# Expert gates of a PEER layer: one-hot products on TensorE replaced by indirect adds into DRAM tables

## The chip, the cores and the metric

The kernel runs on one core of a Trainium2 chip. The metric is the device time of one execution in microseconds (us), the median of several runs. An engine is a processor of the core with its own instruction queue: TensorE (PE, with its weight loads as PEld), VectorE (DVE), ScalarE (ACT), GpSimd (POOL) and SyncE (SP). SP and POOL also issue DMAs, which run on the core's 16 DMA engines.

## What is computed

Three layers in turn each end in a PEER feed-forward block over 256 tokens of width 1024. The rest of a layer (convolution, RWKV, gated linear attention, memory attention, norms) is not touched by the change. The block, cut to what matters:

```python
q = (xb @ w_q).reshape(TOK, 8, 2, 128)                   # 8 heads, 2 halves
s = einsum('thcd,hcnd->thcn', q, sub_keys)               # 128 sub-keys a half
top_s, top_i = top_k(s, 16)
best_s, best_c = top_k((top_s[:,:,0,:,None] + top_s[:,:,1,None,:]).reshape(TOK, 8, 256), 16)
e = i1 * 128 + i2                                        # 8 x 16 experts of 16384 for a token
gate = softmax(best_s)                                   # within a head
act = gelu(einsum('td,ted->te', xb, expert_u[e]))
y = einsum('te,ted->td', gate * act, expert_v[e])
```

An expert may be chosen by several heads of one token; its gates then add up. Within one head the 16 experts are distinct. All values are float32.

## The kernel before, in words

Instead of fetching chosen experts, the kernel multiplies all 16384 experts: 128 blocks of 128 experts. The function `peer` runs, for each layer, three stages:

- The query stage: 16 blocks of `w_q` are streamed (`pq`), scores are formed on PE (`pscore`) and copied to `S`.
- The up stage: a loop over 128 blocks `b` of `uT`. Each step streams 512 KB, splits it into a high and a low part (`hi` on ACT, L75; `lo` on DVE, L77), does 24 matmuls into `pu` (L91 to L93), and puts Gelu of the result into `C3[:, b]`, a table of 128 (expert in block) x 128 blocks x 256 tokens in SBUF.
- The down stage: a loop over 128 blocks of `v` (`vstep`, then `acc_nat`). Each step streams 512 KB, splits it the same way, splits `C3[:, b]` into `ch` (ACT, L86) and `cl` (DVE, L87), and does 12 matmuls of 512 columns into `py` (L142 to L144).

The gates are made by a generator, `background`, which runs beside the query and the up stage. Each piece of it yields a planned cost, and `pull(rate)` is called once a streamed block (14 times in the query stage, then 128 times in the up stage), adding `rate` = 1.3 to a budget that the pieces use up. First it finds the top 16 of every score row (`topk1`, 32 pieces of cost 1.0), then for each half `tt` of 128 tokens the 128 experts and gates (`topk2`, pieces that sum to 20.0). Then, for each group of four tokens, DVE and ACT build one-hot rows `A` (times the gate) and `B`, and PE multiplies them into a gate plane (`pg`, L1075), which multiplies or fills the columns of those four tokens in `C3` (L1079, L1080).

Streams go through `stream`: SP loads `raw` (4 buffers), then `hi` and `lo` (3 buffers each). The order of instructions on each engine is fixed when the program is built: the framework's scheduler puts an instruction where it expects its inputs to be ready, by priority, so that work of a later stage may stand ahead of work of an earlier one. On the chip an engine then keeps this order and waits where an input is not there. `cst` is a pool of constants, `wp` one of work tiles of `peer`, `dr` one of DRAM tiles. GpSimd does little here: a few loads of rows, stores of results and memsets.

Of the kernel before, what the change touches and what calls it, by code (L numbers as in the profile page):

```python
# [6 lines left out]
F32 = mybir.dt.float32  # L7
# [32 lines left out]
class Net:  # L40
    def __init__(self, ctx, nc, tc):
        self.nc, self.tc = nc, tc
        self.cst = ctx.enter_context(tc.tile_pool(name="cst", bufs=1))
        self.sp = ctx.enter_context(tc.tile_pool(name="sp", bufs=PARTS))
        self.xp = ctx.enter_context(tc.tile_pool(name="xp", bufs=1))
        self.ps = ctx.enter_context(tc.tile_pool(name="ps", bufs=2, space=PSUM))
        iota_i = self.sp.tile([128, 128], I32, tag="raw", name="iota_i", bufs=RAW)
        nc.gpsimd.iota(iota_i, pattern=[[1, 128]], base=0, channel_multiplier=0)
        self.iota = self.cst.tile([128, 128], F32, name="iota")
        nc.vector.tensor_copy(self.iota, iota_i)  # L50
        col_i = self.sp.tile([128, 1], I32, tag="raw", name="col_i", bufs=RAW)
        nc.gpsimd.iota(col_i, pattern=[[0, 1]], base=0, channel_multiplier=1)
        self.col = self.cst.tile([128, 1], F32, name="col")
        nc.vector.tensor_copy(self.col, col_i)
        self.ident = self.cst.tile([128, 128], F32, name="ident")
        self.ready = nc.vector.tensor_scalar(self.ident, self.iota, self.col, None, op0=OP.is_equal)

        self.vec2 = self.mark = None
        self.los = []
        self.eps = {}  # L60
        for e in (RMS_EPS, LN_EPS, GN_EPS):
            t = self.cst.tile([128, 1], F32, name=f"eps{len(self.eps)}")
            nc.vector.memset(t, e)
            self.eps[e] = t
        warm = self.cst.tile([128, 1], F32, name="warm")
        nc.scalar.activation(warm, self.eps[RMS_EPS], AF.Sqrt)


    def stream(self, ap, n=1024):
        nc = self.nc  # L70
        raw = self.sp.tile([128, n], F32, tag="raw", name="raw", bufs=RAW)
        nc.sync.dma_start(raw, ap)
        hi = self.sp.tile([128, n], F32R, tag="hi", name="hi")
        lo = self.sp.tile([128, n], F32R, tag="lo", name="lo")
        nc.scalar.copy(hi, raw)  # L75
        with self.behind():
            self.los.append(nc.vector.tensor_tensor(lo, raw, hi.bitcast(F32), op=OP.subtract))  # L77
        return hi, lo

    def behind(self):  # L80

# [152 lines left out]
    def block1(self, a, xh_out, xl_out, stop=None):  # L234
# [5 lines left out]
        with ExitStack() as ctx:  # L240
# [35 lines left out]
            for n, i in enumerate((4, 5, 6, 7, 12, 13, 0, 1, 2, 3, 8, 9, 10, 11)):  # L276
# [6 lines left out]
                S.activation(zf[:, i], pz, AF.Copy, scale=omu[:, i:i + 1])  # L283
                V.scalar_tensor_tensor(zf[:, i], z[:, 0:272], vc("mu", i), zf[:, i], op0=OP.mult, op1=OP.add)
            r_, k_, v_ = zf[:, 0:4], zf[:, 4:8], zf[:, 8:12]
            with tc.issue_after(self.los[5].ins):
                m = self.bmask(mp, f1)
            h64s = mp.tile([128, 128], F32, name="h64s")
# [735 lines left out]
            po = self.proj_nat(a["b_w_out"], fh, fl_, (6, 7, 0, 1, 2, 3, 4, 5))  # L1024
            self.add_ln(fp, res, po, a, (1, 0), xh_out, xl_out, dst)

    def peer(self, xh, xl, wq, skT, uT, v, rate=1.3, dve_a=2):


        nc, tc = self.nc, self.tc  # L1030
# [2 lines left out]
        with ExitStack() as ctx:  # L1033
# [12 lines left out]
            eq = scr(4096, 1024)  # L1046
            views = [self.topk_views(s_) for s_ in small]

            state = {"ub": 0, "tok": 0}

            def background():
                for g in range(16):
                    for tt in range(2):
                        yield from self.topk1(views[tt], S[tt], tmp, 2 * g + tt)
                idT = []
                for tt in range(2):
                    r = yield from self.topk2(wp, views[tt], cand[tt], tmp, eq)
                    idT.append(r)
                for t0 in range(0, 256, 4):
                    tt = t0 // 128  # L1060
                    t1 = t0 - tt * 128
                    A = wp.tile([128, 4, 128], F32, tag="A", name="A")
                    B = wp.tile([128, 4, 128], F32, tag="B", name="B")
                    pg = self.ps.tile([128, 4, 128], F32, tag="y", name="pg", bufs=4)
                    V.tensor_tensor(B, self.iota[:, None, :].to_broadcast([128, 4, 128]),  # L1065
                                    idT[tt][:, 1, t1:t1 + 4, None].to_broadcast([128, 4, 128]), op=OP.is_equal)
                    for j in range(4):
                        t = t1 + j
                        i1, gg = idT[tt][:, 0, t:t + 1], idT[tt][:, 2, t:t + 1]
                        if j < dve_a:  # L1070
                            V.tensor_scalar(A[:, j], self.iota, i1, gg, op0=OP.is_equal, op1=OP.mult)
                        else:
                            nc.scalar.activation(A[:, j], self.iota, AF.Abs, bias=idT[tt][:, 3, t:t + 1])
                            nc.scalar.activation(A[:, j], A[:, j], AF.Relu, scale=idT[tt][:, 4, t:t + 1], bias=gg)  # L1074
                        nc.tensor.matmul(pg[:, j], B[:, j], A[:, j], start=True, stop=True)  # L1075
                    pT = pg.rearrange("p t b -> p b t")
                    n = state["ub"]
                    if n < 128:
                        nc.scalar.copy(C3[:, n:, t0:t0 + 4], pT[:, n:])  # L1079
                    V.tensor_tensor(C3[:, :n, t0:t0 + 4], C3[:, :n, t0:t0 + 4], pT[:, :n], op=OP.mult)  # L1080
                    state["tok"] = t0 + 4
                    yield 0.6 + 0.26 * dve_a + 0.06 + 0.00416 * n

            bg = background()
            debt = [0.0]
# [16 lines left out]
            def score(g, qT):  # L1102
# [4 lines left out]
                for tt in range(2):  # L1107
                    nc.scalar.copy(S[tt][:, g], pg[:, tt])

            for g in range(16):  # L1110
                hi, lo = self.stream(wq[g])
                if g == PARTS:
                    self.mark = None
                pa = self.ps.tile([128, 512], F32, tag="a", name="pq", bufs=4)
                if g < 2:
                    self.mm8(pa[:, :256], hi, lo, xh, xl)
                else:
                    for c in range(8):
                        s = slice(c * 128, c * 128 + 128)
                        self.mm3(pa[:, :256], hi[:, s], lo[:, s], xh[:, c], xl[:, c], c == 0, c == 7)  # L1120
                if g:
                    score(g - 1, qT)
                qT = wp.tile([128, 256], F32, tag="act", name="qT")
                nc.scalar.copy(qT, pa[:, :256])
                if g > 1:
                    pull(rate)
            score(15, qT)
            for b in range(128):
                pull(rate)
                hi, lo = self.stream(uT[b])  # L1130
                pa = self.ps.tile([128, 512], F32, tag="a", name="pu", bufs=4)
                for c in range(8):
                    s = slice(c * 128, c * 128 + 128)
                    self.mm3(pa[:, :256], hi[:, s], lo[:, s], xh[:, c], xl[:, c], c == 0, c == 7)
                tm = state["tok"]
                if tm < 256:
                    nc.scalar.activation(C3[:, b, tm:], pa[:, tm:256], AF.Gelu)
                if tm > 0:
                    act = wp.tile([128, 256], F32, tag="act", name="act")
                    nc.scalar.activation(act[:, :tm], pa[:, :tm], AF.Gelu)  # L1140
                    V.tensor_tensor(C3[:, b, :tm], C3[:, b, :tm], act[:, :tm], op=OP.mult)
                state["ub"] = b + 1
            pull(1e9)
            py = [self.ps.tile([128, 512], F32, tag="y", name="py", bufs=4) for i in range(4)]
            def vstep(b):
                hi, lo = self.stream(v[b])
                ch = wp.tile([128, 256], F32R, tag="ch", name="ch", bufs=TAIL)
                cl = wp.tile([128, 256], F32R, tag="cl", name="cl", bufs=TAIL)
                self.split(ch, cl, C3[:, b])
# [26 lines left out]
        self.top16(w["tv"][:, g], w["ti"][:, g], S[:, g], tmp[:, (i % 8) * 128:(i % 8) * 128 + 128])  # L1176
        yield 1.0

    def topk2(self, wp, w, cand, tmp, eq):

# [51 lines left out]
        sm = t[:, 0:8]  # L1234
        V.tensor_reduce(sm, gt, axis=AX.X, op=OP.add)
        V.reciprocal(sm, sm)
        V.tensor_tensor(gt, gt, sm[:, :, None].to_broadcast([128, 8, 16]), op=OP.mult)
        pt = self.ps.tile([128, 512], F32, tag="y", name="pt", bufs=4)
        for i in range(3):
            nc.tensor.transpose(pt[:, i * 128:i * 128 + 128], pick[:, i], self.ident)  # L1240
        idT = wp.tile([128, 5, 128], F32, tag="idT", name="idT")
        nc.scalar.copy(idT[:, 0:3].rearrange("p a b -> p (a b)"), pt[:, :384])
        V.tensor_scalar(idT[:, 3], idT[:, 0], -1.0, None, op0=OP.mult)
        V.tensor_scalar(idT[:, 4], idT[:, 2], -1.0, None, op0=OP.mult)
        yield 1.0
        return idT


def blk(w):
# [70 lines left out]
def build(nc, tc, a):  # L1320
    with ExitStack() as ctx:
# [3 lines left out]
        n.dr = dr  # L1325
        hs = [dr.tile([256, 1024], F32, name=f"h{i}") for i in range(3)]
        a["h1"] = hs[0]

        def xt():
            return [n.xp.tile([128, 8, 256], F32R, tag="x" + x, name="x" + x) for x in "hl"]  # L1330

        def peer(l, x):
            return n.peer(*x, a[f"wq{l}"], a[f"sk{l}"], a[f"u{l}"], a[f"v{l}"])
        x = xt()
        n.block1(a, *x)
        nc.gpsimd.dma_start(n.vec2, a["vec2"])
# [36 lines left out]
```

## Time and profile before

| what | value |
|---|---|
| median of 3 runs | 3102.98 us (3101.91 to 3103.67) |
| the profiled execution | 3102.61 us, of which the span of the trace is 3100.8 us |
| PE busy | 3044.2 us (98% of the span) |
| DVE, ACT, POOL busy | 2200.1 us (71%), 1763.2 us (57%), 30.6 us (1%) |
| DMA | 518.33 MB, mean 167 GB/s |

Busy times are of one profiled execution. Matmuls overlap in the engine, so that a matmul's own duration is longer than the time by which it moves the next one; a stretch divided by the count of its matmuls gives the latter.

### The profile page before, as it was taken

To read this page: it belongs to the slowest core of one execution; us is meant where nothing else is said; L and a number is where in the kernel's file an instruction comes from. 1 tells how busy PE (TensorE), PEld (TensorE's weight loads), DVE (VectorE), ACT (ScalarE), POOL (GpSimd) and SP (SyncE) were. 2 spreads that over 40 slices of the span, in tenths; PEclk is the share of its full clock that TensorE was granted. 3 is DMA by queue.
4 is the path that set the end of the run, shared out by engine and by line. 5 is a ranking of instruction groups with operands and counts; after the bars stand their busy time and mean duration, and the time that the engine had idled before them with its cause. 6 is when DMAs were issued, how large, how long until landed. Compare 5 with 4: busy or idle time off the path is not lost.

```text
span 3100.8 us, 57093 instructions
## 1 busy us (share of the span) xinstructions
PE 3044.2 (98%) x22090; PEld 2798.0 (90%) x22090; DVE 2200.1 (71%) x4412; ACT 1763.2 (57%) x3433; POOL 30.6 (1%) x83
## 2 busy tenths in 40 slices
PE   9999999999999999999999999999999999999998
PEld 8888999999888878899999988888889999988887
DVE  6977997776666665798777566666599877756666
ACT  6345558775454554456777445456545677645454
POOL 0010000000000010000000000000000000000000
PEclk9999999999999999999999999999999999999999
DMA  5145554445666553455444565555345544455655
GB/s 180 37 153 191 182 183 144 144 150 165 195 192 195 192 177 116 159 188 170 143 144 150 178 196 191 196 192 173 118 166 182 163 144 143 150 190 193 194 192 175
DMA packets 142832, 518.33 MB, mean 167 GB/s; under 512 B 16048, under 2 KB 16320, under 8 KB 142304
## 3 DMA queue, kind: packets, MB, share of 16 engines
q1 hardware_dynamic: 139424, 504.13, 50.2%
q0 software_dynamic: 3136, 10.55, 0.9%
q8 instruction: 173, 2.83, 0.4%
q14 instruction: 99, 0.81, 0.1%
HBM read 508.33 MB, written 6.29 MB: 166 GB/s over the span
## 4 chain that ended last, share of the span: by engine, by line
PE 91%; DVE 5%; DMA 2%; ACT 2%; issue 1%; POOL 0%; DVEq 0%; SPq 0%; ACTq 0%; POOLq 0%
PE pu L92 12%; PE pu L91 12%; PE pu L93 12%; PE py L142 11%; PE py L143 11%; PE py L144 11%; PE pg L1075 6%; PE pz L91 2%; PE pz L93 2%; PE pz L92 2%; DVE acc L318 1%; PE pq L93 1%; PE pq L92 1%; PE pq L91 1%; DVE lo L77 1%
## 5 line engine op out<-in xcount | busy, mean ns | idle before, releaser
L77 DVE TENSOR_TENSOR lo<-raw,hi 128x1024 fp32r<-128x1024 f32 (+1 forms) x939 | 1141.3, 1216 | 444.5 <-ACT hi L75 443.4
L75 ACT CAST hi<-raw 128x1024 fp32r<-128x1024 f32 (+1 forms) x939 | 978.9, 1043 | 621.1 <-PE pu L92 405.1
L91 PE MATMUL pu<-xh,hi 128*128 128x256 f32 x3072 | 885.3, 288 | 0.0
L92 PE MATMUL pu<-xl,hi 128*128 128x256 f32 x3072 | 868.8, 283 | 0.0
L93 PE MATMUL pu<-xh,lo 128*128 128x256 f32 x3072 | 868.8, 283 | 0.0
L143 PE MATMUL py<-lo,ch 128*128 128x512 f32 x1536 | 597.9, 389 | 0.0
L144 PE MATMUL py<-hi,cl 128*128 128x512 f32 x1536 | 597.6, 389 | 0.0
L142 PE MATMUL py<-hi,ch 128*128 128x512 f32 x1536 | 597.4, 389 | 0.0
L92 PEld LDWEIGHTS pu<-xl,hi 128*128 128x128 f32 x3072 | 589.0, 192 | 0.0
L91 PEld LDWEIGHTS pu<-xh,hi 128*128 128x128 f32 x3072 | 588.4, 192 | 0.0
L93 PEld LDWEIGHTS pu<-xh,lo 128*128 128x128 f32 x3072 | 588.1, 191 | 0.0
L86 ACT CAST ch<-C 128x256 fp32r<-128x256 f32 x384 | 156.1, 407 | 514.3 <-PE py L143 507.9
L143 PEld LDWEIGHTS py<-lo,ch 128*128 128x128 f32 x1536 | 288.3, 188 | 60.5 <-DVE lo L77 0.8
L144 PEld LDWEIGHTS py<-hi,cl 128*128 128x128 f32 x1536 | 288.3, 188 | 60.0
L142 PEld LDWEIGHTS py<-hi,ch 128*128 128x128 f32 x1536 | 288.1, 188 | 60.2 <-ACT hi L75 0.9
L87 DVE TENSOR_TENSOR cl<-C,ch 128x256 fp32r<-128x256 f32 x384 | 163.1, 425 | 204.6 <-ACT ch L86 204.6
L1065 DVE TENSOR_TENSOR B<-iota,idT 128x512 f32<-128x512 f32 x192 | 132.5, 690 | 132.6 <-PE pg L1075 132.6
L1075 PE MATMUL pg<-A,B 128*128 128x128 f32 x1536 | 202.7, 275 | 0.0
L1075 PEld LDWEIGHTS pg<-A,B 128*128 128x128 f32 x1536 | 188.5, 192 | 0.0
L1074 ACT ACTIVATE A<-A,idT 128x128 f32<-128x128 f32 x384 | 169.0, 493 | 0.1
L91 PE MATMUL pz<-xh,hi 128*128 128x256 f32 (+1 forms) x504 | 149.2, 297 | 8.6 <-ACT hi L75 5.9
L93 PE MATMUL pz<-xh,lo 128*128 128x256 f32 (+1 forms) x504 | 147.2, 293 | 1.3 <-DVE lo L77 1.3
(482 smaller groups left out, 3549.9 us busy)
## 6 DMA issues: line engine op xcount, KB each, us to landing
raw<-in_u_dram SPq DMA_DIRECT2D x384, 512.0 KB, 3.5
raw<-in_v_dram SPq DMA_DIRECT2D x384, 512.0 KB, 3.5
raw<-in_wq_dram SPq DMA_DIRECT2D x48, 512.0 KB, 3.5
raw<-in_w_in_dram SPq DMA_DIRECT2D x38, 512.0 KB, 4.1
raw<-in_a_w_inT_dram SPq DMA_DIRECT2D x14, 512.0 KB, 3.5
raw<-in_b_wT_dram SPq DMA_DIRECT2D x14, 512.0 KB, 3.5
raw<-in_w_o_dram SPq DMA_DIRECT2D x8, 512.0 KB, 4.4
raw<-in_a_w_out_dram SPq DMA_DIRECT2D x8, 512.0 KB, 3.5
```

What stands on the lines that cost most here:

```text
L75: nc.scalar.copy(hi, raw)
L77: self.los.append(nc.vector.tensor_tensor(lo, raw, hi.bitcast(F32), op=OP.subtract))
L86: nc.scalar.copy(hi, src)
L87: nc.vector.tensor_tensor(lo, src, hi.bitcast(F32), op=OP.subtract)
L91: mm(out, lh, rh, start=start, stop=False)
L92: mm(out, lh, rl, start=False, stop=False)
L93: mm(out, ll, rh, start=False, stop=stop)
L142: mm(po[q], xh[:, ts], hi[:, h], start=f, stop=False)
L143: mm(po[q], xh[:, ts], lo[:, h], start=False, stop=False)
L144: mm(po[q], xl[:, ts], hi[:, h], start=False, stop=l)
L1074: nc.scalar.activation(A[:, j], A[:, j], AF.Relu, scale=idT[tt][:, 4, t:t + 1], bias=gg)
L1075: nc.tensor.matmul(pg[:, j], B[:, j], A[:, j], start=True, stop=True)
```

## The change

Two DRAM tables for each layer, one per half of the tokens, hold one float32 for every expert and token (8 MB each, `G`). They are cleared by SP from a tile of zeros, in pieces of 256 KB (64 a layer): `stream` issues such pieces behind its own load, up to `share` of them a stream (3 in the first layer's mixer, where layer 0's tables are cleared; 0.5 in an up stage, where the next layer's are). `topk2` now leaves gates `gts` and table positions `idx` (128 tokens x 128 choices). For each of the 128 choices of a half, GpSimd issues one indirect DMA that adds 128 values of 4 bytes to the table, one from each partition. The 16 of a head need not wait for each other; those of the next head wait for all 16. The down stage reads the tables back, by GpSimd, in two loads of 256 KB for every four blocks (tile `gate`, 2 buffers), and DVE multiplies `C3[:, b]` by it ahead of the split. `A`, `B`, `pg` and the products with `C3` are gone, as are the transposes of `topk2`. `pull` gets rate 1.55 in place of 1.3.

```diff
+        self.zero = self.cst.tile([128, 512], F32, name="zero")
+        nc.gpsimd.memset(self.zero, 0.0)
...
         nc.sync.dma_start(raw, ap)
+        self.chore(self.share)
...
+    def chore(self, n):
+        self.due += n
+        while self.due >= 1 and self.chores:
+            self.chores.pop(0)()
+            self.due -= 1
+        self.due = min(self.due, 1.0)
+
+    def clear(self, G):
+        assert not self.chores
+        for g in G:
+            v = g.rearrange("(p n) o -> p (n o)", p=128)
+            for i in range(32):
+                self.chores.append(lambda d=v[:, i * 512:i * 512 + 512]: self.nc.sync.dma_start(d, self.zero))
...
+            self.clear(a["G"][0])
+            self.share = 3
             with tc.issue_after(self.los[5].ins):
...
-    def peer(self, xh, xl, wq, skT, uT, v, rate=1.3, dve_a=2):
+    def peer(self, xh, xl, wq, skT, uT, v, G, Gnext=None, rate=1.55):
...
-                for t0 in range(0, 256, 4):
...
-                    V.tensor_tensor(B, self.iota[:, None, :].to_broadcast([128, 4, 128]),
...
-                        nc.tensor.matmul(pg[:, j], B[:, j], A[:, j], start=True, stop=True)
...
-                        nc.scalar.copy(C3[:, n:, t0:t0 + 4], pT[:, n:])
-                    V.tensor_tensor(C3[:, :n, t0:t0 + 4], C3[:, :n, t0:t0 + 4], pT[:, :n], op=OP.mult)
...
+                    yield from self.topk2(views[tt], cand[tt], tmp, eq, idx, gts)
+                    for h in range(8):
+                        now = []
+                        for k in range(16 * h, 16 * h + 16):
+                            i = nc.gpsimd.indirect_dma_start(
+                                G[tt], bass.IndirectOffsetOnAxis(ap=idx[:, k:k + 1], axis=0), gts[:, k:k + 1], None,
+                                compute_op=OP.add)
+                            for j in now:
+                                tc.declare_no_dep(i.ins, j.ins, reason="distinct experts of a head")
+                            after(i, tt)
+                            now.append(i)
+                        last[tt] = now
...
+            while self.chores:
+                self.chore(1)
+            if Gnext is not None:
+                self.clear(Gnext)
+                self.share = 0.5
             for b in range(128):
                 pull(rate)
...
+                nc.scalar.activation(C3[:, b], pa[:, :256], AF.Gelu)
             pull(1e9)
...
+            Gv = [g.rearrange("(p b t) o -> p b (t o)", p=128, t=128) for g in G]
             def vstep(b):
+                if b % 4 == 0:
+                    gate[0] = wp.tile([128, 2, 4, 128], F32, tag="gate", name="gate", bufs=2)
+                    for tt in range(2):
+                        after(nc.gpsimd.dma_start(gate[0][:, tt], Gv[tt][:, b:b + 4]), tt)
                 hi, lo = self.stream(v[b])
+                c = C3[:, b].rearrange("p (x t) -> p x t", x=2)
+                V.tensor_tensor(c, c, gate[0][:, :, b % 4], op=OP.mult)
                 ch = wp.tile([128, 256], F32R, tag="ch", name="ch", bufs=TAIL)
```

`after(i, tt)` makes `i` wait for the DMAs of the last head of half `tt`.

## Rows read from the trace of the kernel before

**Rows 1.** The page: busy time, share of the span and instructions of each engine.
```profile
PE 3044.2 (98%) x22090; PEld 2798.0 (90%) x22090; DVE 2200.1 (71%) x4412; ACT 1763.2 (57%) x3433; POOL 30.6 (1%) x83
```

**Rows 2.** The page: the chain that ended last, shares by engine and line.
```profile
PE 91%; DVE 5%; DMA 2%; ACT 2%; issue 1%; POOL 0%; DVEq 0%; SPq 0%; ACTq 0%; POOLq 0%
PE pu L92 12%; PE pu L91 12%; PE pu L93 12%; PE py L142 11%; PE py L143 11%; PE py L144 11%; PE pg L1075 6%; PE pz L91 2%; PE pz L93 2%; PE pz L92 2%; DVE acc L318 1%; PE pq L93 1%; PE pq L92 1%; PE pq L91 1%; DVE lo L77 1%
```

**Rows 3.** Tiles pu, py, pg, first layer: ns min/median/max, first and last start.
```profile
L91 PEld LDWEIGHTS pu<-xh,hi x1024: 188/192/192, 341.8 to 768.2; 128*128 128x128 f32 x171
...
L142 PEld LDWEIGHTS py<-hi,ch x512: 186/188/192, 768.5 to 1116.2; 128*128 128x128 f32 x171
...
L1075 PE MATMUL pg<-A,B x512: 272/275/275, 461.3 to 725.3; 128*128 128x128 f32 x171
```

**Rows 4.** Windows: stretch, busy us (count) by engine, granted clock, DMA share, GB/s.
```profile
0.00:260.00 260.00, 244.14 (x3430) 230.25 (x3431) 201.67 (x392) 128.44 (x208) 14.22 (x59) 0.97 0.41 135
...
378.00:450.00 72.00, 72.00 (x603) 72.00 (x602) 68.30 (x178) 40.35 (x62) 0.00 (x0) 1.00 0.56 183
450.00:740.00 290.00, 290.00 (x2459) 290.00 (x2458) 216.76 (x424) 212.46 (x555) 0.00 (x0) 1.00 0.46 148
740.00:757.00 17.00, 17.00 (x144) 17.00 (x143) 9.36 (x12) 7.92 (x12) 0.00 (x0) 1.00 0.57 187
757.00:1090.00 333.00, 333.00 (x1517) 277.74 (x1516) 200.90 (x244) 166.50 (x246) 0.00 (x0) 1.00 0.60 193
```

**Rows 5.** Timeline of DVE at the up stage's end: start, us, line, idle before.
```profile
728.28 0.76 DVE L87 TENSOR_TENSOR cl<-C,ch 128x256 fp32r<-128x256 f32 x2 [0.47 <-ACT ch L86]
...
730.68 0.42 DVE L1141 TENSOR_TENSOR C<-C,act 128x256 f32<-128x256 f32 x1
...
735.25 1.23 DVE L77 TENSOR_TENSOR lo<-raw,hi 128x1024 fp32r<-128x1024 f32 x1 [1.32 <-ACT hi L75]
...
758.28 1.23 DVE L77 TENSOR_TENSOR lo<-raw,hi 128x1024 fp32r<-128x1024 f32 x1 [1.32 <-ACT hi L75]
```

**Rows 6.** Tile idT, which topk2 writes at its end: durations, first and last start.
```profile
L1242 ACT COPY idT<-pt x6: 471/472/473, 415.9 to 2432.2; 128x384 f32<-128x384 f32 x6
```

**Rows 7.** Groups of POOL by form: busy us, mean ns, idle before.
```profile
L301 POOL DMA_DIRECT2D gates<-gt x16 | 8.7, 541 | 170.2 <-ACT gt L300 170.2
L674 POOL TENSOR_SCALAR res<-tgr,rs 128x1024 f32<-128x1024 f32 x2 | 5.7, 2852 | 4.8 <-DVE rs L164 4.8
...
L281 POOL MEMSET z<- 128x1 f32 x14 | 1.2, 96 | 31.7 <-DVE zf L284 27.9 <-DVE pi L205 3.9
```

**Rows 8.** Timeline of POOL between the first two layers.
```profile
1109.81 0.53 POOL L647 DMA_DIRECT2D rowg<-in_g_final_row_dram  x1 [827.89 <-DVE cl L87]
1110.44 0.53 POOL L647 DMA_DIRECT2D rowb<-in_ln_rows_dram  x1
```

**Rows 9.** DMA: queues (packets, MB, share), then issues with us to landing.
```profile
q1 hardware_dynamic: 139424, 504.13, 50.2%
...
raw<-in_u_dram SPq DMA_DIRECT2D x384, 512.0 KB, 3.5
...
h<-h1t POOLq DMA_DIRECT2D x2, 512.0 KB, 3.0
```

**Rows 10.** Tile gates: its POOL stores (ns), then the time to landing.
```profile
L301 POOL DMA_DIRECT2D gates<-gt x16: 539/539/557, 172.9 to 236.8; - x16
...
DMA to landing us min/median/max: 2.0/3.9/5.8
```

**Rows 11.** Timeline of the down stage, ACT and DVE: start, us, line, idle before.
```profile
899.52 1.05 ACT L75 CAST hi<-raw 128x1024 fp32r<-128x1024 f32 x1
...
900.60 1.23 DVE L77 TENSOR_TENSOR lo<-raw,hi 128x1024 fp32r<-128x1024 f32 x1 [0.53 <-ACT hi L75]
...
901.92 0.41 ACT L86 CAST ch<-C 128x256 fp32r<-128x256 f32 x1 [1.36 <-PE py L143]
...
902.24 1.05 ACT L75 CAST hi<-raw 128x1024 fp32r<-128x1024 f32 x1
```

More of the change, by code (lines that the diff above doesn't have):

```diff
@@ L59, in __init__ @@
         self.los = []
+        self.zero = self.cst.tile([128, 512], F32, name="zero")
+        nc.gpsimd.memset(self.zero, 0.0)
+        self.chores, self.share, self.due = [], 0, 0.0
         self.eps = {}
@@ L1047, in peer, with after @@
             views = [self.topk_views(s_) for s_ in small]
-            state = {"ub": 0, "tok": 0}
+            SYNC = mybir.DependencyInfo(mybir.DependencyClass.Sync, mybir.DependencyReason.DATA)
+            last = [[], []]
+            def after(i, tt):
+                for j in last[tt]:
+                    tc.add_manual_dep(i.ins, j.ins.name, SYNC, reason="adds of the head before")
             def background():
@@ L1054, in background @@
                         yield from self.topk1(views[tt], S[tt], tmp, 2 * g + tt)
-                idT = []
                 for tt in range(2):
-                    r = yield from self.topk2(wp, views[tt], cand[tt], tmp, eq)
-                    idT.append(r)
-                for t0 in range(0, 256, 4):
[L1060 to L1064, printed above, removed]
-                    V.tensor_tensor(B, self.iota[:, None, :].to_broadcast([128, 4, 128]),
[L1066 to L1074, printed above, removed]
-                        nc.tensor.matmul(pg[:, j], B[:, j], A[:, j], start=True, stop=True)
-                    pT = pg.rearrange("p t b -> p b t")
-                    n = state["ub"]
-                    if n < 128:
-                        nc.scalar.copy(C3[:, n:, t0:t0 + 4], pT[:, n:])
-                    V.tensor_tensor(C3[:, :n, t0:t0 + 4], C3[:, :n, t0:t0 + 4], pT[:, :n], op=OP.mult)
-                    state["tok"] = t0 + 4
-                    yield 0.6 + 0.26 * dve_a + 0.06 + 0.00416 * n
@@ new lines, in background @@
+                    idx = wp.tile([128, 128], U32, tag="idx", name="idx")
+                    gts = wp.tile([128, 128], F32, tag="gts", name="gts")
+                    yield from self.topk2(views[tt], cand[tt], tmp, eq, idx, gts)
[10 more added lines that the diff above has]
+                        last[tt] = now
@@ L1108, in score @@
                     nc.scalar.copy(S[tt][:, g], pg[:, tt])
+            self.share = 3
             for g in range(16):
@@ L1134, in peer @@
                     self.mm3(pa[:, :256], hi[:, s], lo[:, s], xh[:, c], xl[:, c], c == 0, c == 7)
[L1135 to L1142, printed above, removed]
+                nc.scalar.activation(C3[:, b], pa[:, :256], AF.Gelu)
             pull(1e9)
             py = [self.ps.tile([128, 512], F32, tag="y", name="py", bufs=4) for i in range(4)]
+            Gv = [g.rearrange("(p b t) o -> p b (t o)", p=128, t=128) for g in G]
+            gate = [None]
             def vstep(b):
+                if b % 4 == 0:
+                    gate[0] = wp.tile([128, 2, 4, 128], F32, tag="gate", name="gate", bufs=2)
+                    for tt in range(2):
+                        after(nc.gpsimd.dma_start(gate[0][:, tt], Gv[tt][:, b:b + 4]), tt)
                 hi, lo = self.stream(v[b])
+                c = C3[:, b].rearrange("p (x t) -> p x t", x=2)
+                V.tensor_tensor(c, c, gate[0][:, :, b % 4], op=OP.mult)
                 ch = wp.tile([128, 256], F32R, tag="ch", name="ch", bufs=TAIL)
@@ L1177, in topk1, with topk2 @@
         yield 1.0
-    def topk2(self, wp, w, cand, tmp, eq):
+    def topk2(self, w, cand, tmp, eq, idx, gts):
         nc = self.nc
@@ L1236, in topk2 @@
         V.reciprocal(sm, sm)
[L1237 to L1244, printed above, removed]
+        V.tensor_tensor(gts.rearrange("p (h k) -> p h k", k=16), gt, sm[:, :, None].to_broadcast([128, 8, 16]),
+                        op=OP.mult)
+        V.tensor_scalar(pick[:, 0], pick[:, 0], 128.0, self.col, op0=OP.mult, op1=OP.add)
+        V.scalar_tensor_tensor(pick[:, 0], pick[:, 1], 16384.0, pick[:, 0], op0=OP.mult, op1=OP.add)
+        V.tensor_copy(idx, pick[:, 0])
         yield 1.0
-        return idT
 def blk(w):
@@ L1327, in build @@
         a["h1"] = hs[0]
+        a["G"] = [[dr.tile([128 * 128 * 128, 1], F32, name=f"G{l}{tt}") for tt in range(2)] for l in range(3)]
         def xt():
@@ L1332, in peer @@
         def peer(l, x):
-            return n.peer(*x, a[f"wq{l}"], a[f"sk{l}"], a[f"u{l}"], a[f"v{l}"])
+            return n.peer(*x, a[f"wq{l}"], a[f"sk{l}"], a[f"u{l}"], a[f"v{l}"], a["G"][l],
+                          a["G"][l + 1] if l < 2 else None)
         x = xt()
```

## The prediction, made before the changed kernel was run

> **What bounds the kernel now.** The engines' totals come first: PE is busy 98% of the span, DVE 71%, ACT 57%, POOL 1% [rows 1]. A pipelined PE can look busy while it waits, so the chain of waits is read next: 91% of it is PE work, and pg, the one-hot product that the change takes out, is 6% by itself [rows 2]. The tile views then give the stages. In the first layer the up stage runs from 341.8 to the first py at 768.5, so 426.7 us, and pg lies in its second part, 461.3 to 725.3 [rows 3]. The other two layers have the same length. The windows show that PE has no gap there: 290 of 290 us busy in the stretch with pg, 17 of 17 behind it, 333 of 333 in the down stage, at a granted clock of 1.00 [rows 4]. So in both stages each us of PE work removed is a us gained, until another engine, a DMA or the adds set the pace.
>
> **What goes.** Without pg an up step takes (758.28 - 735.25) / 8 = 2.88 us [rows 5], so 128 steps take 368.6 us. The stage takes 426.7, and the difference, 58.1 us a layer, is what 512 pg matmuls hold PE up. Three layers: 174.3 us. The 6% of the chain agrees. The building of A and B, the copies into C3 and the Gelu's detour through act go from DVE and ACT; they lay under PE, which was full, and bring nothing more.
>
> **The top-k at rate 1.55.** Between 378 and 450 us, 25 steps, DVE was busy 68.3 of 72 us [rows 4]: 2.73 a step, 1.23 of it lo [rows 5]. The other 1.50 is top-k at rate 1.3; at 1.55 it is 1.79, and DVE needs 3.02 for a step of 2.88. The pieces cost 72 units, 72 / 1.55 = 46.5 pulls, 14 of them in the query stage. 46.5 x 0.14 = 6.5 us a layer, of which the three hi and lo buffers hide some; between 0 and 6.5 I take 5, so 15 in all. That the planned costs give the time is seen in the last topk2's and the first one's end: 52 / 1.3 - 14 = 26 steps or 75 us into the up stage, against 415.9 - 341.8 = 74.1 [rows 3, 6].
>
> **The adds.** The first half's gates are now ready after 52 / 1.55 - 14 = 19.5 steps of 3.02, 59 us into the up stage. Then POOL issues 256 indirect DMAs in 16 heads; it takes p for each, and at each head waits until the last of the one before has landed, L after its issue. They end at 59 + 256 p + 16 (L - p). The up stage ends at 368.6 + 5 = 373.6. For L, a POOL store to DRAM landed after 3.0 us at 512 KB [rows 9], the gates after 2.0 to 5.8 [rows 10]; I take 3.0. No row shows an indirect DMA, so p is bounded. Below: a plain DMA of 128 rows holds POOL 0.54 us [rows 7], and an indirect one does all that and reads 128 indices. Above: far rows only. POOL's slowest per element is the tensor_scalar, 2852 ns for 1024 elements, 2.8 ns each [rows 7]; 128 indices handled once at that rate add 0.36 us (0.90), twice 0.71 (1.25). The extreme is each index as POOL's smallest instruction, 96 ns [rows 7]: 12.8 us. I take 1.0, nearest to the plain DMA plus one pass over the indices: 59 + 256 + 32 = 347, 27 us before the up stage ends. So the adds cost nothing, covered by the up stage's PE work. With that cover gone each further 0.1 us of p is 24 us a layer, 72 in all. They are just hidden at p = 1.11, and the gain is used up near p = 1.32.
>
> A rule speaks against this part. The Trainium skill, "DMA: Bandwidth & Descriptors", section "Rules for kernel authors", says that transfers under 64 KB pay mostly overhead and should be joined; its SWDGE section puts the fixed part at about 2.0 us. If each add paid that one after another, 512 us, the adds would end some 200 us late and I estimate 3550 us. The trace speaks against paying in series: POOL issued two DMAs 0.63 us apart, without waiting for the first to land [rows 8].
>
> What is queued behind a late add: on POOL the first read of the table, then the other reads and the row loads of the next layer; on DVE the first product with the gates, and behind it lo and cl of every later down step; then PE.
>
> **The clears and the DMA engines.** 64 pieces of 256 KB a layer. In the first mixer the DMA engines are busy 0.41 [rows 4], and three pieces behind a load make the next one wait for 768 KB; loads of 512 KB land in 3.5 us [rows 9] and are issued buffers ahead. Between 0 and some 10 us I take 5. In an up stage they add a quarter of the bytes: share 0.57 becomes 0.71 [rows 4]. The adds bring each DMA engine 256 x (8 + 1) = 2304 tiny packets, at between nothing (by bytes) and the mean packet's 0.502 x 16 x 3100.8 / 139424 = 0.179 us [rows 9]. The room, 0.29 x 369 = 107 us, covers 0.046 us each, in the third layer, without clears, 0.069. I take a value under that, nearer to the bytes; cost nothing.
>
> **The down stage.** The product is a DVE operation of 0.42 us, like the one on act [rows 5]. DVE then needs 1.23 + 0.42 + 0.42 of a step of 348.4 / 128 = 2.72 us, with the stage from 768.5 to 1116.9. The table's reads take the DMA share from 0.60 to 0.75 and POOL 2 x 0.54 every four steps. Both are covered by PE, if the product is queued a step ahead. I count 1 us a layer for the first read, 3 in all. The zero tile's memset at the start lies on an idle POOL.
>
> **Sum.** 3102.6 (the profiled execution: span 3100.8, and 1.8 around it) - 174.3 + 15 + 5 + 3 = 2951; the median lies 0.4 above the profiled one, so 2952.
>
> **Rivals.**
>
> *The adds end late (B to break-even, C beyond).* Same mechanism, p above 1.11. For it: nothing shows that POOL handles 128 scattered addresses at the price of one regular pattern. Against: plain DMAs cost 0.54 whatever they move. At p = 1.25 they end 33 us late a layer: 2952 + 100 = 3052. C is the rival on the other side: at p = 1.5 they end 94 us late, 2952 + 282 = 3234; it decides from p = 1.32. One way to get there: an add's start is held up while DVE runs lo, 1.23 of each 2.88 us, a mean wait of 0.43 x 0.61 = 0.26, so p = 1.26 and some 3060 us. The Trainium skill, "SBUF — State Buffer", section "Who interferes with whom", states such a block for a DVE instruction with two SBUF inputs against a GpSimd one that reads SBUF. The 16 stores of gates held POOL 539 to 557 ns [rows 10], so plain issues were not held up; whether reading the index is, no run here shows. This way counts under B.
>
> *D, the DMA engines set the pace.* At 0.09 us a tiny packet, adds and clears together go 100 us over in two layers and 48 in the third: 2952 + 248 = 3200. From 0.076 on it is slower. For: the share of 0.71. Against: the bytes are few.
>
> *E, queue order.* The scheduler put two cl of the down stage ahead of the last 13 up steps' lo [rows 5]. If it expects the adds sooner than they are, DVE stands at a product of the down stage with up steps still behind it. Queued as for p = 0.54 (59 + 138 + 39 = 236) while they end at 347, a layer loses 111 us: 2952 + 333 = 3285.
>
> *F, a loop between ACT and DVE in the down stage.* ch is now queued between hi(b) and hi(b+1) on ACT [rows 11] and waits for the product. If that is queued behind lo(b): hi starts at 899.52, lo at 900.60, the product ends about 902.2, ch follows, and hi(b+1) comes 0.32 after ch's start [rows 11], near 902.56. A step of 3.04 instead of 2.72 costs 41 us a layer: 3075. Against: the product can run up to eight steps ahead, and ACT idles 1.36 a step [rows 11].
>
> **How the numbers follow.** Hidden as forecast 0.36 (own range 2930 to 2985); B 0.14; F 0.05; D 0.10, half of it still faster; C 0.24; E 0.07; within 0.2% (6 us, about what a measurement can tell from no change) 0.04. Faster: 0.36 + 0.14 + 0.05 + 0.05 = 0.60; same 0.04; slower: 0.24 + 0.07 + 0.05 = 0.36. Low end 2925, the sum without the 23 us of costs that I added. High end 3260: p just over 1.5, D at its example; beyond it lie the tail of C, most of E and the extremes of p, some 0.15.
>
> **What would show it.** POOL's mean per indirect DMA (1.0, and under 1.11), and the last add's end against the first py. No pg; up steps of 2.88 behind the top-k, near 3.0 in it; PE without a gap ahead of the first py; down steps of 2.72. A long wait of DVE's product for gate, with PE idle, makes it wrong, and whether it stands before or after the last lo of the up stage tells C from E; up steps longer than 2.88 with ACT waiting for raw tell D.

## The result, and the profile after

The kernel with the change takes 4152.17 us (median; 4147.97 to 4153.21), against 3102.44 us for the kernel before, measured beside it. The ratio is 1.338, with a 95% interval of 1.336 to 1.341. The forecast of 2952 us has the wrong sign, and the time is far above the range's end of 3260.

The page of the changed kernel, totals and slices of the span in tenths (POOL's 768 indirect DMAs are in its busy time):

```profile
PE 2899.2 (70%) x20536; PEld 2638.3 (64%) x20536; DVE 1972.4 (48%) x3773; ACT 1445.4 (35%) x2251; POOL 1437.2 (35%) x1044
PE   8999930008999999992000999999999000199998
DVE  7969510006566666950000656655794000165666
POOL 0001888772000000288877200000038887620000
PEclk9999975559999999996555999999999555599999
DMA  9975632228655543563222865564356222386555
```

PE, which had no gap before [rows 4], now stands still in three stretches of three or four slices. POOL is at 7 to 8 tenths there, the DMA engines at 2, and the clock granted to TensorE falls to 5 tenths. So the loss is three stalls, one a layer, and POOL works in them. The tiles `pu` and `py` in the first layer give the stages (duration min/median/max, first and last start):

```profile
L111 PEld LDWEIGHTS pu<-xh,hi x1024: 188/192/338, 348.4 to 1118.8; 128*128 128x128 f32 x171
L162 PEld LDWEIGHTS py<-hi,ch x512: 186/188/192, 1119.1 to 1466.8; 128*128 128x128 f32 x171
```

The up stage takes 1119.1 - 348.4 = 770.7 us where it took 426.7 [rows 3]; in the other layers 769.4 and 778.0. These three lose 344 + 343 + 351 = 1038 of the 1049 us by which the profiled executions differ. The down stage, from its first `py` start to its last, is as long as before: 347.7.

The groups that carry the adds and what waited behind them (busy, mean ns, idle time before):

```profile
L113 PE MATMUL pu<-xh,lo 128*128 128x256 f32 x3072 | 881.6, 287 | 1182.6 <-DVE lo L81 1182.2
L1092 POOL DMA_INDIRECT G<-gts,idx x768 | 1303.1, 1697 | 638.3 <-issue 268.7
L1171 DVE TENSOR_TENSOR C<-C,gate 128x256 f32<-128x256 f32 x384 | 144.5, 420 | 1224.8 <-DMA gate<-G 1224.1
```

An add holds POOL for 1.697 us on average, and ahead of nearly every one some 0.30 us pass that no wait explains. The waits name the chain: DVE's product with the gates (L1171) waits for the table, PE for `lo`, ACT for the product (us in total, times, longest):

```profile
DVE C L1171 <- DMA gate<-G: 1224.1, 53, 390.8
PEld pu L113 <- DVE lo L81: 1193.5, 54, 386.0
ACT ch L106 <- DVE C L1171: 1164.8, 6, 389.4
```

PE waits in `pu`, an up-stage tile, so at the first layer's stall the up stage is not over. DVE's timeline shows why:

```profile
551.50 1.23 DVE L81 TENSOR_TENSOR lo<-raw,hi 128x1024 fp32r<-128x1024 f32 x1 [1.65 <-ACT hi L79]
943.54 0.42 DVE L1171 TENSOR_TENSOR C<-C,gate 128x256 f32<-128x256 f32 x1 [390.82 <-DMA gate<-G]
943.88 1.22 DVE L81 TENSOR_TENSOR lo<-raw,hi 128x1024 fp32r<-128x1024 f32 x1
```

Between two `lo` of the up stage stands the first product of the down stage, and it waits 390.82 us for the table. The trace has 40 `lo` on DVE between the end of the second `topk2` (L1266, at 442.51) and this product, and 57 up steps still to come behind it: the scheduler had put it there.

The windows give the two rates of the adds and the state of the engines (columns as in rows 4; POOL is the fifth busy time with its count):

```profile
402.00:450.00 48.00, 45.40 (x367) 44.16 (x366) 45.06 (x129) 23.10 (x34) 38.58 (x21) 1.00 0.71 173
450.00:552.00 102.00, 102.00 (x852) 102.00 (x851) 43.39 (x36) 47.52 (x72) 83.42 (x35) 1.00 0.68 186
552.00:938.00 386.00, 7.38 (x62) 7.17 (x60) 0.72 (x1) 1.33 (x2) 313.34 (x204) 0.51 0.23 4
1119.10:1467.00 347.90, 347.90 (x1536) 287.70 (x1535) 210.12 (x254) 173.70 (x254) 1.07 (x2) 1.00 0.59 195
```

While up steps run, POOL gets 35 adds through in 102 us, one in 2.9 us. In the stall, with next to nothing on the other engines, it gets through 204 instructions, 202 of them adds, in 386 us, one in 1.9 us. The timelines of POOL and DVE, laid beside each other, show both cases (start, duration, idle before):

```profile
519.88 2.58 POOL L1092 DMA_INDIRECT G<-gts,idx  x1 [0.30 <-issue]
522.76 2.58 POOL L1092 DMA_INDIRECT G<-gts,idx  x1 [0.30 <-issue]
744.73 1.54 POOL L1092 DMA_INDIRECT G<-gts,idx  x1 [0.30 <-issue]
782.25 1.54 POOL L1092 DMA_INDIRECT G<-gts,idx  x1 [2.30 <-DMA G<-gts,idx]
```

```profile
519.82 1.23 DVE L81 TENSOR_TENSOR lo<-raw,hi 128x1024 fp32r<-128x1024 f32 x1 [1.65 <-ACT hi L79]
522.70 1.23 DVE L81 TENSOR_TENSOR lo<-raw,hi 128x1024 fp32r<-128x1024 f32 x1 [1.65 <-ACT hi L79]
```

Alone an add takes 1.54 us and the next starts 0.30 later: 1.85. Beside the up steps each one starts 0.06 us behind a `lo`, takes 2.58, and 0.30 later the next one starts, 2.88 after the first, again 0.06 behind a `lo`. The adds have fallen in step with the up stage, one to a step. At a new head the wait was 2.30 us in place of 0.30.

### The profile page after: what moved, and what is told of

Same layout as the page of the kernel before. It is cut to its first block, busy times and chain, and to the rows that moved or that the text cites. A ratio compares the mean times of both kernels' runs of the same rounds, so it can differ in the third digit from the quotient of the medians.

```text
span 4149.4 us, 53495 instructions
## 1 busy us (share of the span) xinstructions
PE 2899.2 (70%) x20536; PEld 2638.3 (64%) x20536; DVE 1972.4 (48%) x3773; ACT 1445.4 (35%) x2251; POOL 1437.2 (35%) x1044
## 5 line engine op out<-in xcount | busy, mean ns | idle before, releaser
L113 PE MATMUL pu<-xh,lo 128*128 128x256 f32 x3072 | 881.6, 287 | 1182.6 <-DVE lo L81 1182.2
L1092 POOL DMA_INDIRECT G<-gts,idx x768 | 1303.1, 1697 | 638.3 <-issue 268.7
L111 PE MATMUL pu<-xh,hi 128*128 128x256 f32 x3072 | 873.5, 284 | 0.2 <-ACT hi L79 0.2
L1171 DVE TENSOR_TENSOR C<-C,gate 128x256 f32<-128x256 f32 x384 | 144.5, 420 | 1224.8 <-DMA gate<-G 1224.1
L1168 POOL DMA_DIRECT2D gate<-G x192 | 104.6, 558 | 393.2 <-DVE C L1171 365.3
```

Source lines behind the costliest of these rows:

```text
L111: mm(out, lh, rh, start=start, stop=False)
L113: mm(out, ll, rh, start=False, stop=stop)
L1092: i = nc.gpsimd.indirect_dma_start(G[tt], bass.IndirectOffsetOnAxis(ap=idx[:, k:k + 1], axis=0), gts[:, k:k + 1], None, compute_op=OP.add)
L1171: V.tensor_tensor(c, c, gate[0][:, :, b % 4], op=OP.mult)
```

## The experiments

**The price alone.** Theory: the price is fixed per instruction, on POOL, and a DVE instruction with two SBUF inputs adds to it. Rivals: the DMA engines or the landing set it, or the 128 indices do. This program holds only groups of 16 small DMAs, some alone and some with one companion.

```diff
+phase(lambda k: P.indirect_dma_start(G, off(k), gts[:, k:k + 1], None, compute_op=OP.add))
+phase(<the same>, lambda i: V.tensor_tensor(z, x, y, op=OP.subtract), 40)
...
+phase(lambda k: P.indirect_dma_start(G, off(k), gts[:, k:k + 1], None, compute_op=OP.bypass))
+phase(lambda k: P.dma_start(Gc[:, k * 128:k * 128 + 1], gts[:, k:k + 1]))
```

> A kernel of its own that leaves the network out: eleven groups of 16 GpSimd DMAs of 128 values of 4 bytes, one group after another. If an indirect add's price is that of making its descriptors from 128 indices on POOL, a group alone takes 1.54 us an add and a plain DMA of the same 128 pieces takes 0.54 us; if the price is that of 4-byte pieces or of the accumulation, the plain one takes as long, or the plain accumulating one does. If DVE's two-input operations hold the add up, the group beside tensor_tensor is above 2 us an add and those beside a one-input max, beside ACT copies and beside 512 KB loads stay at 1.54; if the loads hold it up, only the group beside them grows.

POOL's groups by line. L1375 is the add alone. Beside it ran: L1376 DVE subtracting two SBUF tiles, L1378 DVE's tensor_scalar, L1380 DVE's max of one tile, L1382 ACT copies, L1384 loads of 512 KB. Then, alone: L1389 the add with 64 indices, L1386 an indirect write, L1391 an indirect read, L1387 a plain write of the same 128 values, L1388 that write with accumulation.

```profile
L1376 POOL DMA_INDIRECT G<-gts,idx x16 | 35.3, 2208 | 6.9 <-issue 4.6 <-SPq L1365 2.3
L1378 POOL DMA_INDIRECT G<-gts,idx x16 | 30.3, 1891 | 14.8 <-SPq L1365 10.2 <-issue 4.6
L1375 POOL DMA_INDIRECT G<-gts,idx x16 | 25.0, 1561 | 30.9 <-SPq L1365 26.3 <-issue 4.6
L1380 POOL DMA_INDIRECT G<-gts,idx x16 | 24.8, 1549 | 28.1 <-SPq L1365 23.5 <-issue 4.6
L1382 POOL DMA_INDIRECT G<-gts,idx x16 | 24.8, 1547 | 25.8 <-SPq L1365 21.3 <-issue 4.6
L1384 POOL DMA_INDIRECT G<-gts,idx x16 | 24.8, 1547 | 19.7 <-SPq L1365 15.1 <-issue 4.6
L1389 POOL DMA_INDIRECT G<-gts,idx x16 | 22.6, 1411 | 6.6 <-issue 4.6 <-SPq L1365 2.1
L1386 POOL DMA_INDIRECT G<-gts,idx x16 | 15.4, 960 | 11.2 <-SPq L1365 6.6 <-issue 4.6
L1391 POOL DMA_INDIRECT got<-G,idx x16 | 15.2, 950 | 6.7 <-issue 4.6 <-SPq L1365 2.1
L1388 POOL DMA_DIRECT2D G<-gts x16 | 14.3, 3458 | 2.4 <-issue 2.4
L1387 POOL DMA_DIRECT2D G<-gts x16 | 8.6, 544 | 2.9 <-SPq L1365 1.8 <-issue 1.1
```

The 16 issues of a group have 15 gaps between them, 4.6 / 15 = 0.31 each. The plain write costs 0.54, indirection 0.42 more, and accumulation on top of it 0.59 more. Accumulation by itself is cheaper: the 16 records of L1388 overlap, which makes their mean long, but together they last 14.3 us, 0.89 apiece, 0.35 over the plain write. Half the indices save only 0.15, so most of the price is per instruction. Loads and ACT change nothing: the DMA engines do not set it. DVE with two SBUF inputs does add to it (2.21), with one input in max it doesn't (1.55). The Trainium skill, "SBUF — State Buffer", section "Who interferes with whom", says that a DVE instruction with two SBUF inputs contends with a GpSimd one that reads SBUF, and one with a single input only in its two-port modes; the rows of the subtraction and of max agree. The tensor_scalar, which took 0.69 us for the elements that took max 1.23, lies between (1.89); whether it ran in such a mode, no row here says.

**The queue order.** Theory: part of the loss is that the product stands in the middle of the up stage. Rival: it only moves the wait, and the adds' end alone counts. The product is placed behind the last `lo` of the up stage.

```diff
+            up = self.los[-1].ins
...
-                V.tensor_tensor(c, c, gate[0][:, :, b % 4], op=OP.mult)
+                with tc.issue_after(up):
+                    V.tensor_tensor(c, c, gate[0][:, :, b % 4], op=OP.mult)
```

> The product with the gates is queued on DVE behind the last lo of the up stage; nothing else is changed. If the stall is one of queue order on top of late adds: PE runs the whole up stage (some 369 us), about 112 adds are issued beside it at 2.9 us each, the other 144 behind it at 1.85 and some head waits, and the first py comes about 670 us after the first pu in place of 771: 3850 us. If the order did no harm and the adds alone set the end: 4150 us.

It took 3882.5 us, 270 less. The up steps now run through (first window) and PE stands idle behind them (second):

```profile
349.00:723.00 374.00, 370.93 (x3073) 369.02 (x3072) 211.75 (x403) 174.68 (x263) 274.97 (x116) 1.00 0.65 181
723.00:1003.00 280.00, 0.66 (x6) 0.46 (x4) 1.96 (x6) 1.50 (x3) 219.70 (x145) 0.51 0.22 4
```

The up steps by themselves, with no product among them, are seen here (weight loads of `pu`, first layer):

```profile
L111 PEld LDWEIGHTS pu<-xh,hi x1024: 187/192/193, 348.6 to 722.9; 128*128 128x128 f32 x171
```

The wait for the table stays (928.5 us in all, against 1224.1). So the order is a cost of its own, 270 us of the 1049, and the smaller part. The first `py` comes 654 us after the first `pu` instead of 771, but the down stage takes 375.2 us (1002.9 to 1378.1) instead of 347.7, with gaps on PE in its first 150 us, presumably because its products can no longer run ahead. The difference, 117 - 28 = 89 a layer or 267 in three, is the 270 but for a few us.

**Without the adds.** Theory: the adds are the whole loss, and the rest of the sum holds. Rival: clears, table reads and the new wait cost 40 us or more too. The 256 adds of a layer are left out, so that the gates are zero.

> The indirect adds are left out (the tables stay zero, so the block's output is zero); clears, table reads and products stay. If the adds are all of the loss, the terms of the prediction's sum are left: 2952 us, with down steps of 2.72 and up steps of 2.88. If clears, reads or the queue order around the products cost more than was counted, 2990 us or above.

It took 2975.72 us, 128 under the kernel before, which took 3104.13 beside it. The up stage is 380.4 us (349.2 to 729.6), the down stage 347.7. One thing besides the adds is different here: with no add to wait for, the products are queued earlier. The first runs 15.6 us into the up stage, and 40 of the 128 are over by 478.6, beside the top-k, where the kernel with the adds has none before the stall. A second run of this kind has the top-k at rate 1.3 instead of 1.55.

> As the run without adds, with the top-k at rate 1.3 as before in place of 1.55. If DVE's overrun in the top-k is what lengthened the up stage to 380 us over 128 x 2.88 = 369, the stage falls to some 370 to 373 us and the time from 2976 to about 2950. If the rest is due to the clears, the table reads or the products, it stays at 380 and 2976.

It took 2963.2 us; the first `pu` came 5.6 us later and the up stage fell to 374.7.

**The hold-up by `lo`.** Theory: `lo`, which reads two SBUF tiles, is what stretches an add from 1.85 to 2.88. Rival: another part of the up step does. On top of the queue order, ACT also copies `hi` to PSUM, and `lo` reads it there.

```diff
+            hp = self.ps.tile([128, 512], F32, tag="y", name="hp", bufs=4)
+            nc.scalar.copy(hp, hi.bitcast(F32)[:, h])
+            self.los.append(nc.vector.tensor_tensor(lo[:, h], raw[:, h], hp, op=OP.subtract))
```

> As the run with the product queued later, and in the up stage ACT also copies hi into PSUM, so that DVE's lo has one SBUF input in place of two (two operations of half the width). If lo's two SBUF inputs hold up the adds, these take 1.85 us from one to the next all through and the first py comes about 585 us after the first pu: 3580 us. If the loads or ACT hold them up: as without this edit, 3850 us, or more.

It took 3604.2 us, 278 less than with the order alone. With the up steps running, the adds are back at the price that they have alone (ns min/median/max):

```profile
L1107 POOL DMA_INDIRECT G<-gts,idx x768: 1535/1545/2237, 406.5 to 3207.3; - x192
```

**A cheaper indirect DMA.** Theory: the end follows POOL's price. Rival: the small packets' landing sets it. On top of the queue order the adds become plain indirect writes, so that an expert chosen twice keeps only one gate.

```diff
-                                compute_op=OP.add)
+                                compute_op=OP.bypass)
```

> The kernel with the product queued later, and the indirect DMAs write in place of add (an expert chosen by two heads of a token keeps one gate in place of the sum). If POOL's price of making descriptors sets the end of the adds, this follows the price: 0.96 + 0.30 us alone, held up by lo as before, some 1.7 us in the mean, the first py some 540 us after the first pu in place of 654, 3540 us. If the landing of 4-byte pieces set it, 3880 us as with the adds.

It took 3258.67 us, 624 less than with the adds, and 281 less than I expected. A write also lands sooner than an add (2.1 us after its start in the program of the price, against 3.1), so the time alone would fit the rival too; against the rival stands that within a head the instructions follow each other by POOL's own time plus 0.30, with no wait for a landing. The expectation had one write to an up step, as with the adds. The timelines show two:

```profile
502.20 0.95 POOL L1092 DMA_INDIRECT G<-gts,idx  x1 [0.30 <-issue]
503.46 1.32 POOL L1092 DMA_INDIRECT G<-gts,idx  x1 [0.30 <-issue]
505.09 0.96 POOL L1092 DMA_INDIRECT G<-gts,idx  x1 [0.30 <-issue]
```

```profile
502.72 1.23 DVE L81 TENSOR_TENSOR lo<-raw,hi 128x1024 fp32r<-128x1024 f32 x1 [1.65 <-ACT hi L79]
```

The write at 502.20 is already under way when `lo` starts at 502.72, and isn't held up. The one at 503.46 starts inside `lo`, which ends at 503.95, and ends 0.83 us behind that, at 504.78; it has lost 0.36 us. So what is held up lies near the start of the instruction: 0.83 of its 0.96 us are still to come when `lo` ends. The adds fit this: the one at 519.88 ends 1.41 us behind its `lo`, with 1.41 of its 1.54 still to come. Then 0.30 passes, and the next add starts at 1.71, just past the next `lo`, which comes 1.65 behind the last. That is the lockstep, and it is narrow: 0.06 us less and the add would start no later than `lo`, and the ones seen to do so are not held up. In the kernel with the change four adds start together with a `lo` or up to 0.1 us ahead of it, and they take 1.54 to 1.55; one of them, on POOL, and its `lo`, on DVE (second layer):

```profile
1863.91 1.55 POOL L1092 DMA_INDIRECT G<-gts,idx  x1 [3.04 <-issue]
1863.99 1.23 DVE L81 TENSOR_TENSOR lo<-raw,hi 128x1024 fp32r<-128x1024 f32 x1 [1.65 <-ACT hi L79]
```

**Half the adds.** If POOL has time for 128 adds in an up stage (128 x 2.88 = 369 us at the worst) but not for 256, the first half of the tokens can go through a table and the second stay one-hot on PE. The first half's top-k runs first, and the product stands behind the last `lo`. In the first of these runs, and in the one after it, the scratch of the second selection lies over part of the second half's scores, so that some of its experts are others than the reference's; the work is the same in kind and number.

```diff
-                for tt in range(2):
-                    idx = wp.tile([128, 128], U32, tag="idx", name="idx")
...
+                yield from self.topk2(views[0], cand[0], tmp, eq, idx, gts)
...
+                idT = yield from self.topk2(views[1], cand[1], tmp, eq, wp=wp)
+                for t0 in range(128, 256, 4):
```

> Only the first half of the tokens takes its gates through the table; the second half keeps the one-hot products, all its A rows on DVE. The first half's top-k goes first and the product with the gates is queued behind the up stage. Adds held up by lo at 2.88 us each: 41 + 8 x (16 x 2.88 + 3) = 434 us after the first pu, some 25 behind an up stage of 380 + 28 = 409: about 3130 us, slower than before. If lo does not hold them up: hidden, 3050 us.

It took 3090.14 us, a ratio of 0.9951 (0.9934 to 0.9968) to the kernel before, between the two times expected. The adds did not fall in step (1.97 us in the mean in the first layer), and the last one starts 56 us before the first `py`, so they are hidden. With `lo` reading PSUM in up steps 12 to 103 as well, the adds return to 1.54 us each, but the time rises:

> The same, and in up steps 12 to 103 hi is also copied to PSUM by ACT and lo has one SBUF input. The adds then take some 1.85 to 2.0 us each and end about 320 us after the first pu, hidden behind an up stage of about 409 us: some 18 us a layer are gained, 3050 us, faster than before. If ACT or the shared PSUM banks slow the up stage, 3100 us or more.

3289.46 us, ratio 1.059 (1.057 to 1.061). In the window from 440 to 640 PE is busy only 163.8 of 200 us (200 of 200 would be full). Presumably ACT's second copy and the PSUM buffers that it shares with `pg` cost more than the adds' hold-up did; which of the two was not tried. With a scratch region of its own for the second selection:

> As h1_half (first half of the tokens through a table, 128 adds a layer; second half one-hot; product behind the last up step), but with scratch of its own for the second selection, so that the second half's experts are those of the reference; blocks 64 and up of C are filled only once that selection is done. If the times of h1_half hold, about 3090 us, 0.5% under the kernel before: adds of a mean of 1.6 us that end some 50 us before the first py, up stage about 407 us. Rival: later use of the scratch region holds back the Gelu of blocks 64 on, and the up stage grows by some us: 3100 to 3110, no gain over the kernel before.

3092.05 us, ratio 0.9959 (0.9947 to 0.9971). And with the top-k at rate 1.3:

> h3_half_own_scratch with the top-k at rate 1.3 in place of 1.55. The adds start some 5 up steps (15 us) later and still end before the up stage does; e5_rate13 gained 5.7 us an up stage from the rate and lost 5.6 us once ahead of the first: about 3078 us, 0.8% under the kernel before. Rival: the one-hot part of the second half, which begins later too, runs into the end of the up stage and costs more than the rate gives: 3090 to 3110.

3064.61 us, ratio 0.9871 (0.9856 to 0.9885), the best of all that keep the computation. The adds of the first layer and the up stage's window:

```profile
L1096 POOL DMA_INDIRECT G<-gts,idx x128: 1541/1614/4650, 394.5 to 702.5; - x128
346.00:744.30 398.30, 398.26 (x3337) 397.87 (x3336) 296.48 (x726) 196.26 (x456) 251.76 (x132) 1.00 0.66 173
```

The last add starts 42 us before the first `py` at 744.3, and PE has no gap in the stage. 398.3 is what the removal of half of `pg` should leave: 426.7 - 58.1 / 2 = 397.7. At rate 1.55 PE was busy 401.2 of 406.6. The rate gave 8 us a stage, more than the 5.7 I expected from the run without adds; why it gave more was not tried.

About half of this gain is lost again in the down stage. The three up stages save 85 us, but with the product behind the last `lo` each down stage is about 14 us longer than before, 42 in all, and the first `pu` comes 4 us later; 39 are left of the 85, about the 40 measured. The loss lies at the start of the stage, here beside the same stretch of the kernel with the change:

```profile
744.30:820.00 75.70, 66.45 (x280) 51.03 (x279) 56.70 (x158) 31.38 (x48) 15.03 (x28) 1.00 0.75 251
1119.10:1195.00 75.90, 75.90 (x338) 62.86 (x337) 45.83 (x56) 38.15 (x56) 0.00 (x0) 1.00 0.57 194
```

PE does 280 matmuls there instead of 338. In the first of the runs with half the adds the down stages are 11 to 13 us longer, 35 of the 40 us by which it missed the 3050 for hidden adds. All runs with this placement have such a loss, also the one with writes (26 us a layer); the kernel with the change and the run without adds, which leave the product where the scheduler puts it, have none. Whether half the adds without this placement would keep the whole gain was not tried.

## Why the prediction was wrong, step by step

- **What goes (58.1 us a layer): right.** Without adds the kernel takes 2976, and half of `pg` removed leaves the up stage at 398.3, 0.6 from the step's value.
- **The top-k at rate 1.55 (5 a layer): near, somewhat too small.** In the order run the last weight load shown for `pu` starts 722.9 - 348.6 = 374.3 us after the first, and 0.4 us of the last up step follow, so the 128 steps take 6.1 more than 368.6; in the other layers 8.0 and 8.1. That is 22 us where the sum had 15. The run without adds looks worse, with up stages of 380.4, 382.6 and 382.1, so 39 over; presumably the other 17 come of its early products, which share DVE with the top-k. These 39 instead of 15, 7.4 instead of 5 ahead of the first `pu`, and none of the 3 for the first reads make the 24 us by which the sum without adds is off.
- **The adds, p = 1.0: the step that failed.** Its formula holds to about 1%, counted to the first `py`, which lies 6 to 7 us behind the last add's end: with p as measured, the mean duration and the 0.30 gap, 54 + 256 x (1.927 + 0.30) + 16 x 2.0 is 656 us for the order run, whose first `py` comes 654 after its first `pu`; 58 + 256 x 1.853 + 32 is 564 for the PSUM run (563); 54 + 256 x 1.407 + 32 is 446 for the writes (448). The first add (54 us after the first `pu`, 59 forecast) and the wait at a head (2.0 over an issue) are right too. Where the forecast had p = 1.0, it was 1.85 alone and 2.88 beside `lo`, so that 256 adds could not end in an up stage of 374 us. My near upper end was 1.25, from one POOL rate for 128 elements; the step should not have preferred the row of the plain DMA, since nothing of an indirect one had been seen, and all that lies between 1.32 and the extreme of 12.8 ought to have had more than 0.24.
- **Rival C: the right mechanism, beyond its example.** Its hold-up by `lo` is there but was sized as a mean wait of 0.26. An instruction that falls in step with `lo` pays nearly the whole `lo` each time: 2.58 - 1.54 = 1.04 us. This makes 278 us. But even without it, 1.85 is above the break-even of 1.32, and the kernel, in the better order, takes 3604.
- **Rival E: it came too, on top.** DVE stood at a product of the down stage with 57 up steps behind it (943.5 to 1119.1 is 176 us of work). It costs 270 us beyond the adds' late end; the example in the forecast was 333.
- **Rival D: no.** The DMA engines' share in the stall is 0.23, and in the program of the price loads of 512 KB changed nothing. By an estimate from the stall's window the tiny packets cost 386 x 0.23 / 204 / 9 = 0.048 us each, at the forecast's 9 to a DMA engine and add, near the room of 0.046 that the forecast had left, but the adds come too slowly for it to count.
- **Rival F: no.** Down steps take 347.7 / 128 = 2.72 us, as forecast.
- **The clears (5 us): near, by another way.** All 192 pieces, for all three layers, were issued between 6.7 and 252.8 us, those meant for the up stages too, so none lay in an up stage. The first mixer ran at a DMA share of 0.9, and the first `pu` came 6.6 us later.
- **The rule on small transfers.** The Trainium skill, "DMA: Bandwidth & Descriptors", section "Rules for kernel authors", puts these transfers at mostly overhead; the estimate of 3550 us from the 2.0 us apiece of its SWDGE section lay nearer than the forecast. From start to start the trace shows 1.85. The next add does not wait for the landing of the one before (at a head, where it does, 2.30 us of idle time follow the 1.54), so the series is that of POOL's issuing.

The account, from the run without adds: 2976, + 628 for adds at 1.85 us and the slower start of the down stage behind them (the PSUM run), + 278 for the hold-up by `lo`, + 270 for the order: 4152. These are differences of single runs, so a few us of each mean nothing. The 2976 contain the 17 us of early products, which the other runs do not have; without them the first term would be near 2959 and the second 17 larger.

## What to carry to other kernels

An operation of which the trace has no row, issued hundreds of times, decides the forecast by its price; the row that looks most like it is only its lower bound, and where the break-even lies close above that, most of the chance lies beyond it. Work on an idle engine is hidden only up to that engine's rate beside its neighbours: count how many issues fit into the stage, and move that many (128 of 256 here gave 1.3%). An early consumer of late work belongs behind the last instruction of the stage that covers it, or a queue in fixed order stops that stage too; here that placement in its turn lengthened the next stage, by 11 to 31 us a layer.

## What had not been expected of the hardware

- An indirect accumulating DMA of 128 four-byte values held POOL 1.55 us, an indirect write 0.96, a plain write 0.54; 64 indices instead of 128 saved 0.15.
- The hold-up by DVE strikes an indirect DMA only if it starts inside the DVE instruction (0.95 against 1.32 us for the write), and two repeating sequences of nearly the same period lock: 2.58 + 0.30 = 2.88, the up step.
- In the stalls the granted clock went to 0.51 with PE busy 7 of 386 us; that is the 1.2 GHz level, against 1.00 or 2.4 GHz in the stages. It was 0.50 in the first 4 us of work behind the stall, 0.89 in the next 4 and 1.00 after that, so the return cost 2 us or less a layer.
